# Start addresses of the SBUF tiles in a one-core attention and feed-forward block

## The chip, the cores and the metric

The kernel runs on one core of one Trainium2 chip. The metric is the device time of one execution in microseconds (us), taken as the median of several runs. A profile is one execution, taken by the hardware profiler; its span reaches from the first to the last instruction, and the execution's own time is a little longer than its span.

## The reference

One decoder layer over a sequence of 512 tokens of width 1024, in float32. What is computed, cut to its steps:

```
h    = rms_norm(x)                                   # 512 x 1024
proj = h @ w_in                                      # queries, keys, values and gates of both head groups
A: 4 heads of differential attention: softmax(q1 k1) - lam * softmax(q2 k2), times v, rms_norm
B: 8 heads of sparse attention: compressed blocks + selected blocks + sliding window, mixed by gates
x    = x + rms_norm(concat(A, B) @ w_out)
h    = rms_norm(x)
f    = (silu(h @ w_gate) * (h @ w_up)) @ w_down      # inner width 2816
out  = x + rms_norm(f)
```

With 512 tokens and 8 selectable blocks of which up to 16 are picked, the selected branch and the sliding window both cover the whole causal triangle, so the kernel computes both as plain causal attention.

## The kernel before, in words

Every large product runs on TensorE (PE) in three passes. [...] Weights come from HBM as tiles `wraw` (128x1024, three buffers), ACT makes `whi` (L101, called by `split_w`, L105) and DVE makes `wlo` (L109).

The stages, in order of time:

- Load x, split it into eight `xh` and eight `xl` tiles (L186 to L200).
- Projections: `fm_tile` (L257) holds 24 matmuls of 512 columns into one PSUM bank (L264); `dv_half` and `vg_proj` (L338, L360) have 256 and 280 columns. Rotated queries and keys go to scratch DRAM and come back as `qst` and `kst`.
- Attention heads: scores (L473, L474, with `kst` streamed), softmax on DVE, ACT and POOL, transposes of the probabilities (L489), and the products with the values (L540, L617, L621, with the transposed probabilities `pth`, `ptl`, `pct` streamed).
- Output projection (`mix_part` L664, `mix_final` L676), the residual sum and the second norm, whose transposed result is split into `hth` and `htl` (L807, L808).
- Feed-forward, gate and up (`ff_gate`, L828): for each of 22 blocks of 128 inner columns, 24 matmuls for the gate and 24 for the up half, all in L835.
- Feed-forward, down (`down`, L872): for each of the 22 blocks, 24 matmuls in L874.

[...] In the matmul call the stationary operand comes first and the moving one second:

```
L264  pe.matmul(pt, w[:, k * P:(k + 1) * P], xx[k], ...)                      # moving: xh, xl
L835  pe.matmul(pt, w_col(ww, k), hx[:, k, s0:s1], ...)                       # moving: hth, htl
L874  pe.matmul(acc[i][c], a[f][:, i * P:(i + 1) * P], w[wi][:, c * SEQ:(c + 1) * SEQ], ...)  # moving: whi, wlo
```

For blocks 2 to 21, L835 streams 512 columns at a time (20 x 48 = 960 matmuls); blocks 0 and 1 stream two halves of 256 columns (192 matmuls). The program's order on each engine is set by a scheduler that takes the order of the code, with priorities (`HP`, `HP2`, `HP3`).

SBUF tiles come from pools. A pool takes a stretch of each partition's bytes, and a tile's start follows from what was placed ahead of it, rounded up to 32 bytes. The pools `const`, `weights`, `s` (36 slots of 2048 bytes) and `r` are laid from the low end; `t`, the attention's pool, from the high end; when the attention is done `t` is given back, and `a`, the pool of the feed-forward stage (`hth`, `htl`, the residual `x2`, `silu`, `mixt`), takes its bytes. Small columns (row maxima, row sums, scales, one to 96 floats wide) lie between the wide tiles of `t`.

Of the kernel before, what the change touches and what calls it, by code (L numbers as in the profile page):

```python
# [9 lines left out]
F32 = mybir.dt.float32  # L10
# [7 lines left out]
P = 128  # L18
D_MODEL = 1024
SEQ = 512  # L20
NT = SEQ // P
# [7 lines left out]
NSA_HEADS = 8  # L29
GROUPS = 2  # L30
# [3 lines left out]
NCMP = (SEQ - CMP_BLOCK) // CMP_STRIDE + 1  # L34
NPAD = 32
CMP_HIDDEN = 4 * HEAD_DIM
NLH = CMP_BLOCK // 2
# [40 lines left out]
def hybrid_block_kernel(  # L78
# [8 lines left out]
    def f32(ap):  # L87
        return ap.bitcast(F32)

    cpool = ctx.enter_context(tc.tile_pool(name="const", bufs=1))  # L90
    wpool = ctx.enter_context(tc.tile_pool(name="weights", bufs=3))
    dram = ctx.enter_context(tc.tile_pool(name="scratch", bufs=1, space=bass.MemoryType.DRAM))

    def load_w(src, w=1024):
# [34 lines left out]
    S = ctx.enter_context(tc.tile_pool(name="s", bufs=NS, side="left"))  # L129
    R = ctx.enter_context(tc.tile_pool(name="r", bufs=2, side="left"))  # L130
    tctx = ExitStack()
    T = tctx.enter_context(tc.tile_pool(name="t", bufs=2, side="right"))
    ident = cpool.tile([P, P], F32, name="ident")
    ident_r = T.tile([P, P], F32R, bufs=1, name="ident_r")
    ident_b = T.tile([P, P], BF16, bufs=1, name="ident_b")
    mask_b = T.tile([P, P], BF16, bufs=1, name="mask_b")
    cmask_b = T.tile([P, NT * NPAD], BF16, bufs=1, name="cmask_b")
    sel = T.tile([P, 2 * NCMP], F32, bufs=1, name="sel")
    valid = T.tile([P, 1], F32, bufs=1, name="valid")
    ones = cpool.tile([P, 1], F32, name="ones")  # L140
    gc = cpool.tile([P, NK + 1], F32, name="gc")
    rstd = T.tile([P, NT], F32, bufs=1, name="rstd")
    nrstd = T.tile([P, NT], F32, bufs=1, name="nrstd")
    lam = T.tile([P, 1], F32, bufs=1, name="lam")
    gates = T.tile([P, NT, 3 * NSA_HEADS], F32, bufs=1, name="gates")
    kch = T.tile([P, GROUPS, NPAD], F32R, bufs=1, name="kch")
    kcl = T.tile([P, GROUPS, NPAD], F32R, bufs=1, name="kcl")
    vcs = T.tile([P, GROUPS, HEAD_DIM], F32R, bufs=1, name="vcs")
# [9 lines left out]
    def tslot(name, dt=F32, tag="c"):  # L158
        return T.tile([P, SEQ], dt, tag=tag, name=name, bufs=TAGS[tag])

    def ps(tag, name, dt=F32):
        return PS.tile([P, SEQ], dt, tag=tag, name=name, bufs=PSB[tag])
# [58 lines left out]
    dve.tensor_copy(sel, cst[:, 3 * P:3 * P + 2 * NCMP])  # L221
    dve.tensor_copy(valid, cst[:, 3 * P + 2 * NCMP:3 * P + 2 * NCMP + 1])
    dve.memset(ones, 1.0)
    zero = T.tile([P, GROUPS], F32, bufs=1, name="zero")
    dve.memset(zero, 0.0)
    rp = [sslot(n, F32) for n in ("cos", "sin", "ckv", "skv")]
    cos, sin, ckv, skv = rp
# [16 lines left out]

    lv = sslot("lv", F32)
    nc.sync.dma_start(lv[:, :4 * HEAD_DIM], lamv.partition_broadcast(P))
    l2 = T.tile([P, 2], F32, bufs=1, name="l2")
    for j in range(2):
        dve.tensor_tensor(lv[:, 256 + 64 * j:320 + 64 * j], lv[:, 128 * j:128 * j + 64],
                          lv[:, 128 * j + 64:128 * j + 128], OP.mult)  # L250
# [49 lines left out]
    def load_q(d, m):  # L300
        q = T.tile([P, SEQ], F32R, tag="q", name="qst", bufs=BUFS["q"])
        nc.sync.dma_start(f32(q), d[m].rearrange("d c t -> (d c) t"))
        return q

    def load_k(d, m):
        kk = T.tile([P, 2, SEQ], F32R, tag="k", name="kst", bufs=BUFS["k"])
        src = d[m].rearrange("d (c h) t -> (d c) (h t)", h=2)
        dst = f32(kk).rearrange("(x r) h t -> r x (h t)", r=2)
        for r in range(2):
            nc.sync.dma_start(dst[r], src)  # L310
        return kk
# [63 lines left out]
    def compress(d, v, w1, w2, posd, w2cols):  # L375
        xx = tslot("cx", tag="c")
        nc.sync.dma_start(xx.rearrange("p (g n) -> p g n", g=GROUPS), d[v].rearrange("g d r c n -> (d r c) g n"))
        pos = T.tile([P, NLH], F32, tag="pos", name="pos", bufs=2)
        nc.sync.dma_start(pos, posd.rearrange("(a d) l -> d a l", d=HALF))
        w2t = T.tile([P, 2, w2cols], F32, name=f"w2_{v}", bufs=1)  # L380
        if v:
            nc.sync.dma_start(w2t, w2)
        else:
# [79 lines left out]
    def softmax_map(q, kk, l):  # L463
        ptiles = []
        for grp in ((0, 1), (2,), (3,)):
            st = ps("sc", "sc")
            off = 0
            for i in grp:
                w = (i + 1) * P
                sv = st[:, off:off + w]  # L470
                off += w
                lhs = q[:, i * P:(i + 1) * P]
                pe.matmul(sv, lhs, kk[:, 0, :w], start=True, stop=False)  # L473
                pe.matmul(sv, lhs, kk[:, 1, :w], start=False, stop=False)  # L474
                pe.matmul(sv[:, i * P:], ident_b, mask_b, start=False, stop=True)  # L475
                nm = T.tile([P, 1], F32, tag="nm", name="nm", bufs=8)
                dve.tensor_reduce(nm, sv, AX.X, OP.max, negate=True)  # L477
                pt = T.tile([P, w], F32, tag=f"p{i}", name="p", bufs=PB)
                act.activation(pt, sv, AF.Exp, bias=nm, accum_out=l[:, i:i + 1])  # L479
                ptiles.append(pt)  # L480
        return ptiles
# [14 lines left out]
    def row_mul(eng, p, l):  # L496
        if eng == "p":
            pool.tensor_tensor(p, p, l.to_broadcast(list(p.shape)), OP.mult)  # L498
        elif eng == "a":
            act.activation(p, p, AF.Copy, scale=l)  # L500
        else:
            dve.tensor_scalar(p, p, l, None, OP.mult)

    def new_pt():
        return [T.tile([P, 10, P], F32R, tag="pt" + n, name="pt" + n, bufs=BUFS["pt"]) for n in "hl"]

    def blocks(t, j):
        return t[:, BASE[j]:BASE[j] + NT - j].rearrange("p i q -> p (i q)")
# [9 lines left out]
            nsa_head_(*a)  # L518

    def diff_head_(h, qd, kd, dv):  # L520
        l = T.tile([P, 2, NT], F32, tag="l", name="l", bufs=4)
        pp = []
        for m in range(2):
            mm = 2 * (h % 2) + m
            q, kk = load_q(qd, mm), load_k(kd, mm)
            pp.append(softmax_map(q, kk, l[:, m]))
        dve.reciprocal(l, l)
        dve.tensor_scalar(l[:, 1], l[:, 1], lam, None, OP.mult)  # L528
        pth, ptl = new_pt()
        for i in range(NT):  # L530
            p1, p2 = pp[0][i], pp[1][i]
            row_mul(DSC[i], p2, l[:, 1, i:i + 1])
            dve.scalar_tensor_tensor(p1, p1, l[:, 0, i:i + 1], p2, OP.mult, OP.add)  # L533
        transpose_p(pp[0], pth, ptl)
        av = ps("av", "av")
        n = 0
        for j in range(NT):
            for vi, pt in ((0, pth), (1, pth), (0, ptl)):
                v0 = vi * 256 + (h % 2) * P
                pe.matmul(av[:, j * P:], dv[j][:, v0:v0 + P], blocks(pt, j),  # L540
                          start=(n == 0), stop=(n == 3 * NT - 1))
                n += 1
        o32, sq = tslot("o32", tag="o"), tslot("sq", tag="o")
        act.activation(o32, av, AF.Copy, scale=gc[:, NK:NK + 1])
        act.activation(sq, av, AF.Square)
        ms = ps("tr", "ms")
        for i in range(NT):
            pe.matmul(ms[:, i:i + 1], sq[:, i * P:(i + 1) * P], ones, start=True, stop=True)
        rs = cpool.tile([P, NT], F32, tag="rs", name="rs", bufs=2)
        rsqrt_mean(rs, ms[:, :NT], 1.0 / P)  # L550
        rb = ps(RSB, "rsb")
        for i in range(NT):
            pe.matmul(rb[:, i * P:(i + 1) * P], rs[:, i:i + 1].to_broadcast([P, P]), ident, start=True, stop=True)
        dve.tensor_tensor(sq, o32, rb, OP.mult)
        rs = sq
        oth[h], otl[h] = sslot(f"oh{h}"), sslot(f"ol{h}")
        act.activation(oth[h], rs, AF.Copy, scale=1.0 - LAM_INIT)
        dve.scalar_tensor_tensor(otl[h], rs, 1.0 - LAM_INIT, f32(oth[h]), OP.mult, OP.subtract)

    def cmp_head(h, q, l):  # L560
        g = h // HPG
        st = ps("sc", "scc")
        for i in range(NT):
            o = st[:, i * NPAD:(i + 1) * NPAD]
            pe.matmul(o, q[:, i * P:(i + 1) * P], kch[:, g], start=(i == 0), stop=False)
            pe.matmul(o, q[:, i * P:(i + 1) * P], kcl[:, g], start=False, stop=False)
        pe.matmul(st[:, :P], ident_b, cmask_b, start=False, stop=True)
        sv = st[:, :P].rearrange("p (i n) -> p i n", n=NPAD)
        nm = T.tile([P, NT], F32, tag="nmc", name="nmc", bufs=2)
        bc = [P, NT, NPAD]  # L570
        dve.tensor_reduce(nm, sv, AX.X, OP.max, negate=True)
        c = T.tile([P, P], F32, tag="pc", name="pc", bufs=2)
        cv = c.rearrange("p (i n) -> p i n", n=NPAD)
        dve.tensor_tensor(cv, sv, nm.unsqueeze(2).to_broadcast(bc), OP.add)  # L574
        act.activation(cv, cv, AF.Exp)
        dve.tensor_reduce(l[:, 0], cv[:, :, :NCMP], AX.X, OP.add)
        return c, cv
# [15 lines left out]

    def nsa_head_(h, q, kst, vn, opair):
        g = h // HPG
        l = T.tile([P, 3, NT], F32, tag="l3", name="l3", bufs=4)
        def row_scale(b):
            dve.reciprocal(l[:, b], l[:, b])
            dve.tensor_tensor(l[:, b], l[:, b], gates[:, :, 3 * h + b], OP.mult)
# [284 lines left out]
    for i in range(NT):  # L884
# [3 lines left out]
        u, a, x_ = work("uf"), acc[i], halves(x2[i])  # L888
# [96 lines left out]
```

## Time and profile before

| | |
|---|---|
| median of 3 runs | 717.43 us (714.56 to 718.01) |
| the profiled execution's own time | 715.25 us |
| its span | 713.2 us |
| mean granted TensorE clock | 0.982 |
| PE busy | 683.7 us (96% of the span) |
| DVE busy | 488.3 us (68%) |
| ACT busy | 295.9 us (41%) |
| DMA engines, mean busy share | 35% |

PE is the engine with the highest share, and the share of a whole span is an average over stages. Matmuls overlap one another in the profile (the end of one is modelled, and lies behind the start of the next), so the pace of a stretch of matmuls is read from their starts and their number, not from the duration of one.

### The profile page before, as it was taken

The numbers are of one execution on the slowest core, as the hardware profiler recorded it, in microseconds if no ns is written. First come the engines' busy times: TensorE is split into PE (matmuls) and PEld (weight loads), VectorE is DVE, ScalarE is ACT, GpSimd is POOL, SyncE is SP. The second block draws the span as 40 slices with busy tenths as digits, with TensorE's granted clock in tenths as the row PEclk, the third lists the DMA queues.
The fourth block names the chain that finished last, engine by engine and source line by source line (L and its number), as shares of the span: only waits on it lengthen the run. The fifth ranks groups of instructions, "written<-read, shape, count | busy, mean of one in ns | idle before, by whom it ended". The sixth has DMA issues, their size and how long they took to land.

```text
span 713.2 us, 9399 instructions
## 1 busy us (share of the span) xinstructions
PE 683.7 (96%) x3536; PEld 566.2 (79%) x3536; DVE 488.3 (68%) x803; ACT 295.9 (41%) x612; POOL 63.1 (9%) x74
## 2 busy tenths in 40 slices
PE   7999999999899998987899999999999999999995
PEld 4888878898788877866888888888888888888884
DVE  5777988876999995669586766867667672222227
ACT  7334444466689965435323233232232321121113
POOL 0000000111745434000000000000000000000000
PEclk8999999999999998999999999999999999999999
DMA  8347878551221300470022332223322222322303
GB/s 311 129 133 244 279 238 298 195 191 45 86 78 60 104 16 30 133 251 30 1 90 88 105 102 89 89 88 93 111 92 89 88 91 94 111 89 88 110 8 119
DMA packets 25980, 83.62 MB, mean 117 GB/s; under 512 B 3408, under 2 KB 4304, under 8 KB 25040
## 3 DMA queue, kind: packets, MB, share of 16 engines
q1 hardware_dynamic: 25936, 83.03, 35.0%
q8 instruction: 28, 0.46, 0.3%
q14 instruction: 16, 0.13, 0.1%
HBM read 73.06 MB, written 9.96 MB: 116 GB/s over the span
## 4 chain that ended last, share of the span: by engine, by line
PE 81%; DVE 12%; ACT 4%; issue 2%; DMA 1%; SPq 0%; DVEq 0%; ACTq 0%
PE gu L835 35%; PE acc L874 15%; PE fm L264 11%; PE tr L489 2%; PE mixp L664 2%; DVE nm L477 2%; PE dv L338 2%; PE vg L360 2%; PE avn L617 2%; PE sc L473 2%; PE sc L474 1%; PE mix L676 1%; PE av L540 1%; DVE p L533 1%; DVE ptl L494 1%
## 5 line engine op out<-in xcount | busy, mean ns | idle before, releaser
L109 DVE TENSOR_TENSOR wlo<-wraw,whi 128x1024 fp32r<-128x1024 f32 (+2 forms) x96 | 116.4, 1214 | 144.8 <-ACT whi L101 95.5
L101 ACT ACTIVATE whi<-wraw 128x1024 fp32r<-128x1024 f32 (+2 forms) x96 | 100.8, 1052 | 215.3 <-PE gu L835 92.0
L835 PE MATMUL gu<-hth,whi 128*128 128x512 f32 (+1 forms) x352 | 86.6, 388 | 0.0
L835 PE MATMUL gu<-htl,whi 128*128 128x512 f32 (+1 forms) x352 | 86.2, 385 | 0.0
L835 PE MATMUL gu<-hth,wlo 128*128 128x512 f32 (+1 forms) x352 | 85.6, 385 | 0.0
L835 PEld LDWEIGHTS gu<-hth,whi 128*128 128x128 f32 x352 | 65.0, 192 | 14.8 <-ACT hth L807 0.3
L835 PEld LDWEIGHTS gu<-htl,whi 128*128 128x128 f32 x352 | 64.3, 188 | 14.7
L835 PEld LDWEIGHTS gu<-hth,wlo 128*128 128x128 f32 x352 | 64.1, 188 | 14.7
L841 DVE RECIPROCAL silu<-silu 128x512 f32<-128x512 f32 (+1 forms) x24 | 74.0, 3085 | 0.7
L498 POOL TENSOR_TENSOR p<-p,l 128x384 f32<-128x384 f32 (+3 forms) x60 | 50.1, 862 | 145.0 <-DVE l L528 88.5
L874 PE MATMUL acc<-whi,ffl 128*128 128x512 f32 x144 | 56.0, 389 | 0.0
L874 PE MATMUL acc<-wlo,ffh 128*128 128x512 f32 x144 | 56.0, 389 | 0.0
L874 PE MATMUL acc<-whi,ffh 128*128 128x512 f32 x144 | 55.9, 389 | 0.0
L479 ACT ACTIVATE p<-sc,nm 128x128 f32<-128x128 f32 (+1 forms) x96 | 50.0, 528 | 10.2 <-DVE nm L477 9.8
L477 DVE TENSOR_REDUCE nm<-sc 128x1 f32<-128x128 f32 (+1 forms) x96 | 42.5, 482 | 11.0 <-PE sc L475 7.8
L264 PE MATMUL fm<-xh,whi 128*128 128x512 f32 x128 | 35.9, 419 | 4.8 <-ACT whi L101 2.9
L493 ACT ACTIVATE pth<-tr 128x384 fp32r<-128x384 f32 (+1 forms) x60 | 31.5, 526 | 17.4 <-PE tr L489 17.2
L473 PE MATMUL sc<-kst,qst 128*128 128x128 f32 (+2 forms) x96 | 35.6, 372 | 1.5 <-DVE pc L574 1.2
L494 DVE TENSOR_TENSOR ptl<-tr,pth 128x384 fp32r<-128x384 f32 (+1 forms) x60 | 34.8, 592 | 3.0 <-ACT pth L493 2.7
L489 PE MATMUL tr<-ident,p 128*128 128x128 f32 x200 | 33.6, 280 | 1.3 <-ACT pct L591 0.7
L264 PEld LDWEIGHTS fm<-xh,whi 128*128 128x128 f32 x128 | 24.9, 199 | 12.3 <-ACT whi L101 5.5
L264 PE MATMUL fm<-xl,whi 128*128 128x512 f32 x128 | 32.6, 391 | 0.0
(219 smaller groups left out, 1186.9 us busy)
## 6 DMA issues: line engine op xcount, KB each, us to landing
wraw<-in_wg SPq DMA_DIRECT2D x22, 512.0 KB, 3.3
wraw<-in_wu SPq DMA_DIRECT2D x22, 512.0 KB, 3.3
wraw<-in_wd SPq DMA_DIRECT2D x22, 512.0 KB, 3.3
wraw<-in_wf SPq DMA_DIRECT2D x16, 512.0 KB, 4.9
qk<-rope SPq DMA_DIRECT2D x7, 1024.0 KB, 5.9
kst<-qk SPq DMA_DIRECT2D x24, 256.0 KB, 4.4
qst<-qk SPq DMA_DIRECT2D x16, 256.0 KB, 2.7
wraw<-in_wo SPq DMA_DIRECT2D x8, 512.0 KB, 4.0
```

Source lines behind the costliest of these rows:

```text
L101: act.activation(dst, src, AF.Copy)
L109: (lo_eng or dve).tensor_tensor(lo[:, :w], raw[:, :w], f32(hi[:, :w]), OP.subtract)
L264: pe.matmul(pt, w[:, k * P:(k + 1) * P], xx[k], start=(n == 0), stop=(n == 3 * NK - 1))
L473: pe.matmul(sv, lhs, kk[:, 0, :w], start=True, stop=False)
L477: dve.tensor_reduce(nm, sv, AX.X, OP.max, negate=True)
L479: act.activation(pt, sv, AF.Exp, bias=nm, accum_out=l[:, i:i + 1])
L489: pe.transpose(tr[:, n * P:(n + 1) * P], pts[i][:, j * P:(j + 1) * P], ident)
L494: dve.tensor_tensor(ptl[:, sl], trv, f32(pth[:, sl]), OP.subtract)
L498: pool.tensor_tensor(p, p, l.to_broadcast(list(p.shape)), OP.mult)
L835: pe.matmul(pt, w_col(ww, k), hx[:, k, s0:s1], start=(n == 0), stop=(n == 3 * NK - 1))
L841: dve.reciprocal(sl, sl)
L874: pe.matmul(acc[i][c], a[f][:, i * P:(i + 1) * P], w[wi][:, c * SEQ:(c + 1) * SEQ], start=(first and n == 0), stop=(last and n == 2))
```

## The change

The change moves tiles to other addresses and does nothing else. A pad of 64 bytes (`cpad`) goes into the `const` pool, which moves all tiles of `weights`, `s` and `r`. A pool `edge` with a pad of 224 bytes (`zpad`) is laid at the high end, so that `a` begins lower. A pool `u` takes the small columns out of `t`.

```diff
     cpool = ctx.enter_context(tc.tile_pool(name="const", bufs=1))
+    cpool.tile([P, 16], F32, name="cpad")
     wpool = ctx.enter_context(tc.tile_pool(name="weights", bufs=3))
+    zpool = ctx.enter_context(tc.tile_pool(name="edge", bufs=1, side="right"))
+    zpool.tile([P, 56], F32, name="zpad")
...
     tctx = ExitStack()
+    U = tctx.enter_context(tc.tile_pool(name="u", bufs=1, side="right"))
+    U.tile([P, 32], F32, name="upad")
     T = tctx.enter_context(tc.tile_pool(name="t", bufs=2, side="right"))
...
-    sel = T.tile([P, 2 * NCMP], F32, bufs=1, name="sel")
-    valid = T.tile([P, 1], F32, bufs=1, name="valid")
+    sel = U.tile([P, 2 * NCMP], F32, bufs=1, name="sel")
+    valid = U.tile([P, 1], F32, bufs=1, name="valid")
...
-                nm = T.tile([P, 1], F32, tag="nm", name="nm", bufs=8)
+                nm = U.tile([P, 1], F32, tag="nm", name="nm", bufs=8)
```

In the same way `rstd`, `nrstd`, `lam`, `gates`, `zero`, `l2`, `pos`, `w2_0`, `w2_1`, `l`, `l3` and `nmc` go from `T` to `U`. The starts of the tiles, as the two built programs have them, in bytes above a multiple of 256:

| tiles | pool | before | after |
|---|---|---|---|
| `wraw`, `whi`, `wlo` | weights | 192 | 0 |
| `xh`, `xl`, `dv`, `vn`, `oh`, `ol`, `ws`, `ffh`, `ffl` | s | 192 | 0 |
| `rope` (also the last `ffh`, `ffl`) | r | 192 | 0 |
| `xraw`, `kst`, `pct`, `cst`, `kch`, `vcs` | t | 96 | 0 |
| `qst`, `p`, `pth`, `ptl`, `opair` | t | 160 | 0 |
| `pc` | t | 224 | 0 |
| `hth`, `htl`, `x2`, `gain`, `mixt`, `u`, `silu`, `uf`, `junk` | a | 224 | 0 |
| `ident` (128x128) | const | 160 | 224 |

A slice of such a tile that starts a multiple of 64 columns into it keeps the tile's number, so the moving operands named above start where their tiles start. The lists of instructions of all five engines are the same in both programs, in the same order. What differs is a handful of semaphore waits at the seam between attention and feed-forward, where the pool `a` takes other bytes of `t`: the load of the first gain row waits for a later matmul (the one for which the second gain row, next in SP's queue, waits in both programs), and some waits on loads of `qst` and `kst` stand at other instructions of ACT and DVE.

## Rows read from the trace of the kernel before

**Rows 1.** The page, section 1: busy us, share and count of each engine.

```profile
PE 683.7 (96%) x3536; PEld 566.2 (79%) x3536; DVE 488.3 (68%) x803; ACT 295.9 (41%) x612; POOL 63.1 (9%) x74
```

**Rows 2.** The page, section 4: the chain that ended last, by engine and line.

```profile
PE 81%; DVE 12%; ACT 4%; issue 2%; DMA 1%; SPq 0%; DVEq 0%; ACTq 0%
PE gu L835 35%; PE acc L874 15%; PE fm L264 11%; PE tr L489 2%; PE mixp L664 2%; DVE nm L477 2%; PE dv L338 2%; PE vg L360 2%; PE avn L617 2%; PE sc L473 2%; PE sc L474 1%; PE mix L676 1%; PE av L540 1%; DVE p L533 1%; DVE ptl L494 1%
```

**Rows 3.** The chain in order of time: start us, us, what.

```profile
1.65 4.87 DMA wraw<-in_wf
...
38.63 21.80 PE fm L264 x96
...
348.68 237.28 PE gu L835 x1056
585.96 110.20 PE acc L874 x486
```

**Rows 4.** The timeline of PE, gate and up: start us, us, what.

```profile
425.27 2.03 PE L835 MATMUL gu<-htl,whi 128*128 128x512 f32 x8
427.13 2.03 PE L835 MATMUL gu<-hth,wlo 128*128 128x512 f32 x8
...
432.73 2.03 PE L835 MATMUL gu<-hth,wlo 128*128 128x512 f32 x8
434.60 2.03 PE L835 MATMUL gu<-hth,whi 128*128 128x512 f32 x8
...
438.33 2.03 PE L835 MATMUL gu<-hth,wlo 128*128 128x512 f32 x8
```

**Rows 5.** Groups by line and form, PE: form xcount | busy us, mean ns | idle.

```profile
L835 PE MATMUL gu<-hth,wlo 128*128 128x512 f32 x320 | 81.1, 395 | 0.0
L874 PE MATMUL acc<-whi,ffl 128*128 128x512 f32 x144 | 56.0, 389 | 0.0
```

**Rows 6.** Single lines, PE: count, duration ns min/median/max, first and last start, forms.

```profile
L264 PE MATMUL fm<-xl,whi x128: 389/389/476, 15.8 to 128.3; 128*128 128x512 f32 x128
L621 PE MATMUL avn<-pct,vcs x8: 392/398/405, 188.4 to 298.7; 128*64 128x512 f32 x8
L338 PE MATMUL dv<-whi,xl x64: 279/283/365, 25.6 to 147.8; 128*128 128x256 f32 x64
L835 PE MATMUL gu<-hth,ws x64: 277/283/415, 331.5 to 361.7; 128*128 128x256 f32 x64
```

**Rows 7.** Windows: us; busy PE, PEld, DVE, ACT, POOL; clock; DMA share; GB/s.

```profile
39.00:60.00 21.00, 21.00 (x94) 17.39 (x93) 14.92 (x24) 7.32 (x12) 0.00 (x0) 1.00 0.49 145
400.00:580.00 180.00, 180.00 (x773) 144.57 (x773) 128.74 (x112) 54.07 (x65) 0.00 (x0) 1.00 0.29 94
425.27:427.13 1.86, 1.86 (x9) 1.50 (x8) 1.86 (x1) 0.00 (x0) 0.00 (x0) 1.00 0.66 198
432.60:434.60 2.00, 2.00 (x10) 1.59 (x9) 0.00 (x0) 1.06 (x1) 0.00 (x0) 1.00 0.31 119
```

**Rows 8.** The chain from 125 to 330 us, by line.

```profile
by line: PE tr L489 7.6%; PE mixp L664 7.0%; DVE nm L477 6.7%; PE vg L360 6.3%; PE avn L617 6.2%; PE sc L473 5.1%; PE sc L474 4.2%; PE mix L676 4.0%; PE av L540 3.5%; DVE p L533 3.1%; DVE ptl L494 3.0%; PE dv L338 2.9%; ACT p L479 2.9%; PE 
```

**Rows 9.** Windows as in rows 7: the attention's middle.

```profile
178.00:285.00 107.00, 100.64 (x661) 82.38 (x660) 93.41 (x238) 81.13 (x241) 53.42 (x60) 0.95 0.20 62
```

**Rows 10.** Groups by form, DVE: 1024 elements from tiles of either pool.

```profile
L109 DVE TENSOR_TENSOR wlo<-wraw,whi 128x1024 fp32r<-128x1024 f32 x93 | 113.6, 1223 | 143.9 <-ACT whi L101 94.6 <-PE gu L835 48.3 <-issue 0.6
L793 DVE TENSOR_TENSOR u<-mixt,gain 128x1024 f32<-128x1024 f32 x4 | 4.9, 1222 | 0.0
```

**Rows 11.** DMA issues: line, count, KB each, median us to landing.

```profile
xraw<-in_xT SPq DMA_DIRECT2D x8, 256.0 KB, 5.8
cos<-in_rope SPq DMA_DIRECT2D x1, 256.0 KB, 5.1
```

**Rows 12.** The timeline at the seam: SP's issue of the gain rows, DVE's first use.

```profile
306.51 0.90 SPq L742 DMA_DIRECT2D gain<-in_grow  x2
314.66 1.23 DVE L793 TENSOR_TENSOR u<-mixt,gain 128x1024 f32<-128x1024 f32 x1
```

More of the change, by code (lines that the diff above doesn't have):

```diff
@@ L137, in hybrid_block_kernel @@
     cmask_b = T.tile([P, NT * NPAD], BF16, bufs=1, name="cmask_b")
-    sel = T.tile([P, 2 * NCMP], F32, bufs=1, name="sel")
-    valid = T.tile([P, 1], F32, bufs=1, name="valid")
+    sel = U.tile([P, 2 * NCMP], F32, bufs=1, name="sel")
+    valid = U.tile([P, 1], F32, bufs=1, name="valid")
     ones = cpool.tile([P, 1], F32, name="ones")
     gc = cpool.tile([P, NK + 1], F32, name="gc")
[L142 to L145, printed above, removed]
+    rstd = U.tile([P, NT], F32, bufs=1, name="rstd")
+    nrstd = U.tile([P, NT], F32, bufs=1, name="nrstd")
+    lam = U.tile([P, 1], F32, bufs=1, name="lam")
+    gates = U.tile([P, NT, 3 * NSA_HEADS], F32, bufs=1, name="gates")
     kch = T.tile([P, GROUPS, NPAD], F32R, bufs=1, name="kch")
@@ L223, in hybrid_block_kernel @@
     dve.memset(ones, 1.0)
-    zero = T.tile([P, GROUPS], F32, bufs=1, name="zero")
+    zero = U.tile([P, GROUPS], F32, bufs=1, name="zero")
     dve.memset(zero, 0.0)
@@ L246, in hybrid_block_kernel @@
     nc.sync.dma_start(lv[:, :4 * HEAD_DIM], lamv.partition_broadcast(P))
-    l2 = T.tile([P, 2], F32, bufs=1, name="l2")
+    l2 = U.tile([P, 2], F32, bufs=1, name="l2")
     for j in range(2):
@@ L377, in compress @@
         nc.sync.dma_start(xx.rearrange("p (g n) -> p g n", g=GROUPS), d[v].rearrange("g d r c n -> (d r c) g n"))
-        pos = T.tile([P, NLH], F32, tag="pos", name="pos", bufs=2)
+        pos = U.tile([P, NLH], F32, tag="pos", name="pos", bufs=2)
         nc.sync.dma_start(pos, posd.rearrange("(a d) l -> d a l", d=HALF))
-        w2t = T.tile([P, 2, w2cols], F32, name=f"w2_{v}", bufs=1)
+        w2t = U.tile([P, 2, w2cols], F32, name=f"w2_{v}", bufs=1)
         if v:
@@ L520, in diff_head_ @@
     def diff_head_(h, qd, kd, dv):
-        l = T.tile([P, 2, NT], F32, tag="l", name="l", bufs=4)
+        l = U.tile([P, 2, NT], F32, tag="l", name="l", bufs=4)
         pp = []
@@ L568, in cmp_head @@
         sv = st[:, :P].rearrange("p (i n) -> p i n", n=NPAD)
-        nm = T.tile([P, NT], F32, tag="nmc", name="nmc", bufs=2)
+        nm = U.tile([P, NT], F32, tag="nmc", name="nmc", bufs=2)
         bc = [P, NT, NPAD]
@@ L595, in nsa_head_ @@
         g = h // HPG
-        l = T.tile([P, 3, NT], F32, tag="l3", name="l3", bufs=4)
+        l = U.tile([P, 3, NT], F32, tag="l3", name="l3", bufs=4)
         def row_scale(b):
```

## The prediction

> **What bounds the kernel now.** I read first which engine the end waits for, then the pace of that engine in each stage. PE is busy for 96% of the span [rows 1] and carries 81% of the chain that ended last, DVE 12%, transfers 1% [rows 2]. Three lines hold most of it: L835 (gate and up) 35%, L874 (down) 15%, L264 (projections) 11%. The chain in order of time shows them as unbroken pieces: 21.80 us with 96 matmuls of L264, 237.28 us with 1056 of L835, 110.20 us with 486 of L874 [rows 3]. Inside these pieces PE waits for nobody, so the time of the kernel there is a number of matmuls times the time from one start to the next, which I call the pitch.
>
> The reader is to see that the pitch is not the same in the three lines, though each matmul has 512 moving columns of the same type:
>
> - L264: 21.80 us / 96 = 227.1 ns [rows 3].
> - L874: 110.20 us / 486 = 226.7 ns [rows 3].
> - L835: seven groups of eight start between 425.27 and 438.33 us (the rows in between are of the same kind), so 13.06 us / 56 = 233.2 ns [rows 4].
>
> The durations say the same: 389 ns for L874 [rows 5] and L264 [rows 6], 395 ns for L835 [rows 5]. [...]
>
> Where do 6.3 ns (233.2 less the mean of the other two, 226.9) come from? Not from the other engines. L264 between 39 and 60 us has DVE busy for 14.92 of 21 us (71%), ACT for 35% and DMA for 0.49; L835 between 400 and 580 us has 72%, 30% and 0.29 [rows 7]. Inside L835 the eight matmuls from 425.27 us took 1.86 us with DVE busy throughout, the eight from 432.73 us 1.87 us with DVE idle [rows 4, 7]. Nor from the stationary operand: `whi` and `wlo` serve L264 and L835 alike. What is left in the layout is where the moving operand starts: `xh`, `xl`, `whi` and `wlo` start 192 bytes above a multiple of 256, which is a multiple of 64; `hth` and `htl` start at 224, an odd multiple of 32. A third moving tile, `pct` at 96 (odd again), takes 398 ns at the median, while `xh` and `xl` at 192 take 389 in L264 [rows 6]. So in this trace the clean cases with a start at an odd multiple of 32 cost 6 to 9 ns more per 512 columns. That is a correlation over a handful of tiles. [...]
>
> **The change part by part.** *Feed-forward, gate and up.* `hth` and `htl` go from 224 to 0. If 0 behaves as 192 does, each of the 960 matmuls with 512 columns (three groups like the 320 of [rows 5]) costs 226.9 instead of 233.2 ns: 960 x 6.3 = 6.0 us less. All of it lies on the chain, since the whole stage is one piece [rows 3]. The cover holds: DVE has 128.74 us of work in 180 us [rows 7], and would have it in about 175, 74%. The bounds are 0 (the start has nothing to do with it) and 960 x 9 = 8.6 us (the distance of `pct`); I take 6.0 because both ends of it come from long clean stretches.
>
> *The 192 matmuls with 256 columns in L835*, at the front of the stage: they have a median of 283 ns, and so have the ones of L338, whose moving tiles stand at 192 [rows 6]. With short rows something else sets the pace, and I take 0; the bound above is 192 x 6.3 = 1.2 us.
>
> *Attention.* `kst`, `pth`, `ptl` and `pct` also leave odd multiples of 32. The lines that stream them, L617, L473, L474 and L540, hold 6.2 + 5.1 + 4.2 + 3.5 = 19.0% of the chain between 125 and 330 us [rows 8], so 39 us; 6.3 / 233.2 = 2.7% of that is 1.1 us. In the middle of this stage DVE is busy for 93.41 of 107 us [rows 9] and is what comes late next, and most of these matmuls have fewer than 512 columns. I take half, 0.5 us, and keep 0 and 1.1.
>
> *Projections, output projection, down.* Their moving tiles go from 192 to 0, both multiples of 64: 0. The transposes stream `ident`, which goes from 160 to 224 and stays off: 0. What 0 does that 192 doesn't is shown by no row; the second and third rival are about that.
>
> *DVE, ACT, POOL.* DVE takes 1223 ns for 1024 elements from the tiles at 192 and 1222 ns from those at 224 [rows 10]: 0.
>
> *Transfers.* They are 1% of the chain, the 4.87 us in which the first weights land [rows 3]. The loads of x, into tiles at 96, land after 5.8 us, that of `cos`, into one at 192, after 5.1 [rows 11]; other traffic explains this as well, but as a bound it is 12% of 4.87 us, so 0 to 0.6 us. I take 0, since the two differ in queueing.
>
> [...]
>
> *The waits at the seam.* The first gain row waits for a matmul that its successor in the queue waited for already; the two were issued within 0.90 us at 306.5 us, and DVE first needs one at 314.66 us [rows 12]. The waits that moved on ACT and DVE are for loads of the attention stage, long landed. 0.
>
> **The sum**: 6.0 + 0.5 = 6.5 us. Against the profiled execution that is 713.2 - 6.5 = 706.7 us of span and 715.25 - 6.5 = 708.7 us; this execution lay 2.2 us below the median of the runs, from which the same sum gives 710.9 us. I predict 710.0 us, between the two. For the case's own range I take the upper bounds together, 8.6 + 1.2 + 1.1 + 0.6 = 11.5 us off the profiled execution's 715.25, and for the other end a step a fifth smaller and nothing else, 4.8 us off the median: 704 to 713.
>
> **The rivals.** *Nothing changes* (717.4 us, chance 0.12). The pitch of L835 would then come from something else that only this line has, for instance that its moving tiles are slices of one 16 KB tile. For it speaks that no tile in the trace changes its start while all else stays; against it, that `pct` is slow too and no such slice [rows 6]. [...]
>
> *Slower: one residue for all* (chance 0.06). [...] Priced by the one step the trace shows, the aligned lines would go from 227 to 233 ns: 528 matmuls of L874, 384 of L264 and 192 of L664 and L676, 1104 x 6.3 = 7.0 us, with L835 gaining nothing: 717.4 + 7.0 = 724 us. It decides if L874's pitch rises above 230 ns. Against it: in L264 and L874 all operands stand at 192 already, with DVE 71% busy in the one, and they are the fast lines [rows 3, 7].
>
> *A larger step* (chance 0.08). If 256 (or 128) is a boundary too, all lines gain once more: 528 + 384 + 192 + 960 = 2064 matmuls x 6.3 = 13.0 us on top, 710.9 - 13.0 = 698 us. [...] Against it: nothing in the trace starts at 0 to show it.
>
> That the change misses its aim is no rival here: the built program has the starts that the table gives.
>
> **How the numbers follow.** The forecast has 0.74, nothing 0.12, slower 0.06, the larger step 0.08. A difference of 0.5% (3.6 us) is about what a measurement of this kernel tells from no change. The forecast passes it unless the gain comes out below 3.6 us, for which I leave 0.05 of its 0.74; with 0.08 of the larger step that makes 0.77 for faster, 0.05 + 0.12 = 0.17 for the same, 0.06 for slower. The range 704 to 717 holds the forecast's own and reaches up into the first rival's, whose runs would lie between 714.6 and 718.0 as those of before did; it leaves out the slower case, the larger step and the top of the first rival.
>
> **What would show it.** Right: L835's pitch between 226 and 228 ns and its durations at 389, the chain's long piece of L835 near 231 us instead of 237.28, L874 and L264 unchanged at 227, DVE's forms unchanged. Wrong: L835 still at 233 (the first rival), L874 above 230 (the second), L264 and L874 below 225 (the third), or L835 at 227 with the 6 us given back as new waits of PE in that stage.

## The result and the profile after

| | before | after |
|---|---|---|
| median of the runs timed side by side | 717.12 us (5 runs, 714.56 to 718.01) | 711.54 us (5 runs, 709.9 to 712.37) |
| ratio, 95% interval | | 0.9923 (0.9899 to 0.9946) |
| the profiled execution's own time | 715.25 us | 712.37 us |
| its span | 713.2 us | 710.4 us |
| mean granted TensorE clock | 0.982 | 0.978 |

The kernel became faster by 0.8%, 5.6 us between the medians. The profiled execution of after is the longest of its five, the one of before lies 1.9 us under its median, so the two traces differ by less than the kernels do.

The page of after, section 1 (busy us, share and count of each engine), answers to [rows 1]. PE has 3.6 us less to do; DVE, ACT and POOL are where they were.

```profile
PE 680.1 (96%) x3536; PEld 568.1 (80%) x3536; DVE 488.3 (69%) x803; ACT 296.1 (42%) x612; POOL 62.7 (9%) x74
```

The chain of after in order of time (start us, us, what) answers to [rows 3]:

```profile
39.02 21.80 PE fm L269 x96
...
66.76 7.46 DMA wraw<-in_wf
...
95.86 4.52 PE fm L269 x14
...
353.85 229.41 PE gu L840 x1056
583.26 110.17 PE acc L879 x486
```

L840 is the L835 of before, L879 its L874, L269 its L264. The long piece of gate and up fell from 237.28 to 229.41 us, 7.87 us; down (110.20 to 110.17) and the long piece of the projections (21.80 to 21.80) stayed. But the long piece starts at 353.85 us and not at 348.68: 5.17 us were lost ahead of it, and the span is 2.8 us shorter, not 7.9.

**The gain.** Groups by line and form in after (form xcount | busy us, mean ns | idle), against [rows 5]: gate and up now takes what down takes. A product is summed from `whi` with `xh`, `whi` with `xl` and `wlo` with `xh` (in gate and up `hth` and `htl` in their place), so the line has three groups of 320.

```profile
L840 PE MATMUL gu<-hth,wlo 128*128 128x512 f32 x320 | 79.0, 389 | 0.0
L879 PE MATMUL acc<-whi,ffl 128*128 128x512 f32 x144 | 56.0, 389 | 0.0
```

The timeline of PE in after (start us, us, what), as in [rows 4]:

```profile
425.34 1.98 PE L840 MATMUL gu<-hth,whi 128*128 128x512 f32 x8
...
438.03 1.98 PE L840 MATMUL gu<-htl,whi 128*128 128x512 f32 x8
```

Seven groups of eight lie between these two starts: 12.69 us / 56 = 226.6 ns, where before had 233.2. The window from 400 to 580 us counts the same thing over the whole stage (columns as in [rows 7]): 796 matmuls in 180 us, 773 before. 180 / 796 = 226.1 ns and 180 / 773 = 232.9 ns, at a clock of 1.00 both times.

```profile
400.00:580.00 180.00, 180.00 (x796) 149.05 (x795) 131.60 (x117) 55.96 (x67) 0.00 (x0) 1.00 0.30 97
```

This count is a better measure of the step than the length of the long piece, because the clock at the front of that piece differs between the two executions. Windows from 350 to 355 us, before and then after, have 0.77 and 1.00 (after's long piece begins inside its window):

```profile
350.00:355.00 5.00, 5.00 (x35) 5.00 (x35) 0.61 (x2) 0.21 (x2) 0.00 (x0) 0.77 0.01 3
...
350.00:355.00 5.00, 3.06 (x23) 2.44 (x22) 4.88 (x10) 1.32 (x4) 0.00 (x0) 1.00 0.00 0
```

**The loss ahead of it.** Windows of after (columns as in [rows 7]), in the projections:

```profile
85.00:95.00 10.00, 6.96 (x40) 5.70 (x39) 9.47 (x17) 5.51 (x10) 0.00 (x0) 1.00 0.55 195
95.00:100.00 5.00, 5.00 (x19) 4.12 (x19) 5.00 (x6) 1.84 (x3) 0.00 (x0) 0.66 0.79 233
```

PE was busy for 6.96 of 10 us, and then the granted clock was 0.66 for 5 us; in the window from 95.60 to 98.20 us it was 0.50. The timeline of PE in after shows it in the starts of a row of matmuls: six from 95.66 to 98.22 us, 427 ns each, where the piece of 96 at a clock of 1.00 has 227.1.

```profile
95.66 2.77 PE L269 MATMUL fm<-xh,whi 128*128 128x512 f32 x6
98.22 2.16 PE L269 MATMUL fm<-xl,whi 128*128 128x512 f32 x8
```

In the profile of before the same ten microseconds had PE busy for 8.63 us and the next five a clock of 1.00. The chain tells how much each part cost. The piece of 14 matmuls at 95.86 us in after is this one in before:

```profile
93.06 3.18 PE fm L264 x14
```

So 2.80 of the 5.17 us were lost before this piece (1.67 of them are PE's missing busy time between 85 and 95 us, 8.63 less 6.96), and 1.34 us in it (4.52 against 3.18), at the lower clock. Another 0.9 us came between the first matmuls of gate and up and the long piece, which begins 18.04 us after them in after and 17.14 us in before. Whether the layout has a hand in this is taken up with the runs of the two kernels again.

### The profile page after: what moved, and what is told of

The parts are those of the page before. It is cut to its first block, busy times and chain, and to the rows that moved or that the text cites. A ratio compares the mean times of both kernels' runs of the same rounds, so it can differ in the third digit from the quotient of the medians.

```text
span 710.4 us, 9399 instructions
## 1 busy us (share of the span) xinstructions
PE 680.1 (96%) x3536; PEld 568.1 (80%) x3536; DVE 488.3 (69%) x803; ACT 296.1 (42%) x612; POOL 62.7 (9%) x74
## 4 chain that ended last, share of the span: by engine, by line
PE 79%; DVE 13%; ACT 4%; issue 2%; DMA 2%; DVEq 0%; SPq 0%; ACTq 0%
PE gu L840 34%; PE acc L879 16%; PE fm L269 10%; PE mixp L669 2%; PE tr L494 2%; PE avn L622 2%; PE dv L343 2%; PE vg L365 2%; DMA wraw<-in_wf 2%; PE sc L478 2%; DVE nm L482 2%; PE sc L479 1%; DVE rope L288 1%; PE mix L681 1%; PE av L545 1%
## 5 line engine op out<-in xcount | busy, mean ns | idle before, releaser
L840 PE MATMUL gu<-hth,whi 128*128 128x512 f32 (+1 forms) x352 | 84.3, 382 | 0.0
L840 PE MATMUL gu<-htl,whi 128*128 128x512 f32 (+1 forms) x352 | 84.2, 380 | 0.0
L840 PE MATMUL gu<-hth,wlo 128*128 128x512 f32 (+1 forms) x352 | 83.5, 379 | 0.0
L840 PEld LDWEIGHTS gu<-hth,whi 128*128 128x128 f32 x352 | 64.9, 191 | 12.7 <-ACT hth L812 0.3
L840 PEld LDWEIGHTS gu<-htl,whi 128*128 128x128 f32 x352 | 64.4, 188 | 12.5
L840 PEld LDWEIGHTS gu<-hth,wlo 128*128 128x128 f32 x352 | 64.2, 188 | 12.5
L879 PE MATMUL acc<-whi,ffl 128*128 128x512 f32 x144 | 56.0, 389 | 0.0
L879 PE MATMUL acc<-wlo,ffh 128*128 128x512 f32 x144 | 56.0, 389 | 0.0
L879 PE MATMUL acc<-whi,ffh 128*128 128x512 f32 x144 | 55.9, 389 | 0.0
L269 PE MATMUL fm<-xh,whi 128*128 128x512 f32 x128 | 37.2, 430 | 4.4 <-DVE chl L410 2.1
L269 PEld LDWEIGHTS fm<-xh,whi 128*128 128x128 f32 x128 | 25.7, 206 | 12.3 <-ACT whi L104 5.1
L269 PE MATMUL fm<-xl,whi 128*128 128x512 f32 x128 | 33.2, 396 | 0.0
```

The costliest lines, as they stand in the source:

```text
L269: pe.matmul(pt, w[:, k * P:(k + 1) * P], xx[k], start=(n == 0), stop=(n == 3 * NK - 1))
L840: pe.matmul(pt, w_col(ww, k), hx[:, k, s0:s1], start=(n == 0), stop=(n == 3 * NK - 1))
```

## The experiments

The theory at the start was the prediction's: PE streams a moving operand more slowly when its tile starts at an odd multiple of 32. The first four kernels were timed beside 19 runs of the kernel before (median 716.72 us, 713.82 to 718.35).

**The changed kernel again** (no edit).

> The changed kernel once more, for a second profile. In its first profile the long piece of gate and up is 7.9 us shorter, but the stages ahead of it took 5.2 us more, most of that after a transfer of projection weights that was waited for 7.46 us near 67 us. If that is the scatter of one execution, the start of the long gate-and-up piece comes back towards 349 us here and the time lies at 709 to 712 us. If the new layout slows the transfers of the projection stage, the piece starts at 353 us or later again.

711.15 us (6 runs), ratio 0.9918 (0.9891 to 0.9945): the result holds. The long piece of gate and up took 230.88 us from 353.39 us, which by the words of the expectation speaks for a cost of the new layout; more on that below.

**Only the pool of hth and htl moved.** The kernel before, and 224 bytes laid above `a`; `hth` and `htl` then start at 0 and the weights stay at 192.

```diff
+    Z = ctx.enter_context(tc.tile_pool(name="z", bufs=1, side="right"))
+    Z.tile([P, 56], F32, name="zp")
     A = ...
```

> Only the feed-forward pool is moved (its tiles from 224 to 0 bytes above a multiple of 256); all else is as before. Theory (the start of the moving operand alone): pitch of gate and up 226.7 ns, durations 389 ns, gain 960 x 6.6 = 6.3 us plus what the 256-column matmuls give, so 709 to 711.5 us. Rival (the gain needs moving and stationary operand at the same place above 256): the stationary tiles stay at 192, so the pitch would stay at 233 ns and the time at 717 us.

712.91 us (8 runs), ratio 0.9956 (0.9930 to 0.9982): faster, by something over half of what the whole change gives (two thirds by the medians). The two intervals overlap, so the times alone don't tell the kernels apart. The groups by form do:

```profile
L837 PE MATMUL gu<-hth,whi 128*128 128x512 f32 x320 | 79.9, 392 | 0.0
L837 PE MATMUL gu<-hth,wlo 128*128 128x512 f32 x320 | 79.7, 391 | 0.0
```

391 to 392 ns lie between 395 and 389, and the long piece, 232.84 us, lies between 237.28 and 229.41. A start at 0 alone doesn't bring the full step, which the first theory did not allow for; nor does it stay at 233 ns, as the rival had it.

**Everything else moved, hth and htl left at 224.** The changed kernel, and 32 bytes more above `a`.

```diff
+    Z = ctx.enter_context(tc.tile_pool(name="z", bufs=1, side="right"))
+    Z.tile([P, 8], F32, name="zp")
     A = ...
```

> The change without its feed-forward part: all other tiles at 0, hth and htl back at 224. Theory: pitch of gate and up 233 ns again, time 716 to 718 us, a gain of 0 to 1 us from attention. Rival (the rest of the new layout costs some 2 to 4 us in the projections): 719 to 721 us, and the gate-and-up piece starts at 352 us or later.

716.93 us (12 runs), ratio 1.0001 (0.9987 to 1.0015). `xh`, the weights, `kst`, `qst`, `pth`, `pct`, `ffh` and all loads have their new starts here, and nothing is gained: gate and up is at 396 ns by form, its long piece at 235.62 us.

```profile
L842 PE MATMUL gu<-hth,wlo 128*128 128x512 f32 x320 | 81.1, 396 | 0.0
```

**Everything on the left moved to an odd multiple of 32.** The kernel before with 32 bytes in the `const` pool: the weights and the pools `s` and `r` go from 192 to 224, `hth` and `htl` stay at 224. By the first theory this had to be slower, since down and the projections would now stream from odd starts.

```diff
     cpool = ctx.enter_context(tc.tile_pool(name="const", bufs=1))
+    cpool.tile([P, 8], F32, name="cpad")
```

> The kernel before with 32 bytes of padding in the const pool: weights, activations and split feed-forward tiles go from 192 to 224, an odd multiple of 32, the attention and feed-forward pools stay. Theory: the lines that stream these tiles with 512 columns (down 528, projections 384, output projection 192 matmuls) go from 227 to 233 ns, 1104 x 6.6 = 7.3 us more, 722 to 725 us; gate and up, whose stationary tiles move too, stays at 233. Rival (the stationary start counts as well): gate and up rises above 236 ns, down above 236. Rival (only gate and up's own tiles are special): nothing changes, 717 us.

710.83 us (6 runs), ratio 0.9911 (0.9886 to 0.9936). It is as fast as the changed kernel, with no wide operand of the feed-forward part at a multiple of 64. Single lines of this kernel (duration ns min/median/max):

```profile
L836 PE MATMUL gu<-htl,whi x352: 281/389/389, 335.9 to 577.2; 128*128 128x512 f32 x160, 128*128 128x256 f32 x16
...
L875 PE MATMUL acc<-wlo,ffh x144: 389/389/389, 579.7 to 676.9; 128*128 128x512 f32 x144
```

Here the first theory fell, and no one of the three expectations had a faster kernel. What the five layouts have in common is the distance between the starts of the two operands, the moving one (512 columns here) and the stationary one (the 128x128 part of a tile that an LDWEIGHTS loads): at (192, 192), (0, 0) and (224, 224) a 512-column matmul takes 389 ns; at (0, 192), 64 apart modulo 256, 391 to 392; at (224, 192) and (224, 0), 32 apart, 395 to 396. That is the second theory.

**Other distances.** Three kernels made from the changed one, with `hth` and `htl` cut out of wider tiles so that they start some bytes above the weights' 0; one execution of each. The edit for 64 and 32 bytes (a float has four):

```diff
-    hth = A.tile([P, NK, SEQ], F32R, name="hth")
-    htl = A.tile([P, NK, SEQ], F32R, name="htl")
+    hth = A.tile([P, NK * SEQ + 64], F32R, name="hth")[:, 16:16 + NK * SEQ].rearrange(...)
+    htl = A.tile([P, NK * SEQ + 64], F32R, name="htl")[:, 8:8 + NK * SEQ].rearrange(...)
```

> The changed kernel with hth 64 and htl 32 bytes above a multiple of 256; whi, wlo and all others stay at 0. First theory (only the moving operand's start, boundary at 64): hth 227 ns, htl 233 ns. Second theory (the distance between the moving and the stationary operand's start decides: 0 gives 226.7, 32 gives 233, 64 gives 229): hth 229 ns, htl 233 ns. Durations 392 and 395 ns by the second.

> The changed kernel with hth 16 and htl 4 bytes above a multiple of 256; whi and wlo stay at 0. First theory: both start off a boundary, 233 ns both. Second theory: says only that a distance other than 0 may cost; if distance matters in steps of 32 bytes, both stay at 226.7 ns.

> The changed kernel with hth 128 bytes above a multiple of 256 and htl at 256, which is 0 again; whi and wlo at 0. First theory: both 227 ns. Second theory: htl 226.7 ns; hth between 226.7 (if the pattern repeats every 128 bytes or less) and 230 ns (if it goes on from 64).

The groups by form, `hth` (from `whi`) and `htl` of each. First 64 and 32 bytes (714.91 us):

```profile
L840 PE MATMUL gu<-htl,whi 128*128 128x512 f32 x320 | 81.3, 396 | 0.0
...
L840 PE MATMUL gu<-hth,whi 128*128 128x512 f32 x320 | 79.7, 391 | 0.0
```

16 and 4 bytes (716.14 us):

```profile
L840 PE MATMUL gu<-htl,whi 128*128 128x512 f32 x320 | 82.1, 398 | 0.0
L840 PE MATMUL gu<-hth,whi 128*128 128x512 f32 x320 | 80.6, 394 | 0.0
```

128 and 256 bytes (711.74 us):

```profile
L840 PE MATMUL gu<-hth,whi 128*128 128x512 f32 x320 | 81.2, 395 | 0.0
...
L840 PE MATMUL gu<-htl,whi 128*128 128x512 f32 x320 | 79.6, 391 | 0.0
```

Every distance tried but a multiple of 256 costs something, 4 bytes the most (398), and the cost doesn't fall with the distance: 64 costs less than 128 (391 to 392 against 394 to 395). 32 and 64 give the values that they gave at other places, within one kernel now, as the second theory said. It had left open whether less than 32 bytes counts; it does. Its guess for 128 missed: it allowed up to 230 ns. From 400 to 580 us this kernel has 779 matmuls, 231.1 ns each; two thirds of them are `hth`'s, and with 226 to 228 ns for `htl`'s third the `hth` ones come to some 233 ns, an estimate, as at 32 bytes. At 256 the median is 389 but the mean 391, with single ones up to 398. Each group of eight `htl` matmuls stands between groups at 128; a third of them at 395 and the rest at 389 would make that mean, an estimate again. And in the changed kernel itself `hth` and `whi` start an odd multiple of 256 apart, as the built program has them, and the operands of down an even multiple; both take 389 ns. So 256 is as good as 0. The times are single runs of kernels whose runs spread over 4 us and more, so they decide nothing; the durations do.

**The kernel before again** (no edit).

> The kernel before, for a second profile of its stages. The gate-and-up pitch is 233 ns again. If the first profile was a fast execution ahead of the feed-forward stage, the long gate-and-up piece starts at 350 to 351 us here instead of 348.68; if the changed kernel's layout really costs the projections 4 us, it starts at 348.7 again.

714.18 us, with the long piece of gate and up at 236.64 us from 348.33 us. It was run for the loss ahead of that piece. Windows of this kernel:

```profile
85.00:95.00 10.00, 7.81 (x45) 6.48 (x44) 9.48 (x17) 6.02 (x11) 0.00 (x0) 1.00 0.53 193
95.00:100.00 5.00, 5.00 (x28) 4.25 (x27) 4.22 (x5) 2.24 (x3) 0.00 (x0) 1.00 0.72 218
```

28 matmuls in the five microseconds in which after had 19. By the expectation the start at 348.33 us speaks for a cost of the new layout, and so does the 352.83 us at which the long piece starts with only `hth` and `htl` left at 224; but that kernel's time, 716.93 us against 716.72, shows no such cost. The kernel with 128 and 256 bytes, whose other tiles stand as in the change, has a clock of 1.00 from 70 to 140 us as well:

```profile
70.00:140.00 70.00, 67.88 (x359) 56.56 (x357) 58.40 (x95) 29.68 (x56) 3.52 (x4) 1.00 0.73 256
```

Its long piece starts at 347.90 us. So the layout doesn't force the loss. A late load of weights is not enough for it either. In after that load's piece of the chain ends at 74.22 us (7.46 us from 66.76) and in the kernel before again at 73.39 (6.35 us from 67.04). With everything on the left at 224 it ends at 74.28 us (7.05 us from 67.23), and there the clock stayed at 1.00 from 70 to 140 us. Nor is it always the same loss: the two kernels that follow also start the long piece late, at 352.38 and 353.07 us, with a clock of 1.00 from 70 to 140 us. In their chains a row of eight `rsb` matmuls takes 0.89 us at 164.30 and 165.27 us and 1.72 us at 276.92 and 278.04; in after such a row takes 1.48 us at 278.75, with a clock of 0.83 from 270 to 290 us, and in the kernel before again 0.89 us at 289.25, with a clock of 1.00 from 250 to 300 us. What makes the clock fall in one execution and not in another stays open.

The timed runs span the same clocks, 0.977 to 0.988 for the changed kernel and 0.978 to 0.989 for the one before, and at the upper end the changed one is ahead: 708.13 and 708.44 us at 0.988 against 714.55 and 713.82 at 0.988 and 0.989. Whether the new layout of pool `t` makes such executions more frequent is open. Of the eight profiles taken with it, the two that follow among them, six start the long piece at 352.4 to 353.9 us and two at 347.9 and 350.0; the four taken with the old one start it at 348.3 to 350.3. The times bound it: the kernel with everything on the left at 224 keeps the old `t` and gains 5.9 us (710.83 against 716.72), the changed kernel beside it gains 5.6; and the kernel with only `hth` and `htl` left at 224 has the ratio 1.0001 (0.9987 to 1.0015), so on average the rest of the layout, with what attention may gain by it, costs some 1 us at most.

**The stationary operand moved alone.** Wherever the kernels above moved `hth`, the distance changed with it. Two kernels move the other side. In the first, only the split weights (and the raw tile beside them) go up by 32 bytes: they are the stationary operand of gate and up and of the projections, and the moving one of down.

```diff
+    w0pool = ctx.enter_context(tc.tile_pool(name="w0", bufs=1))
+    w0pool.tile([P, 8], F32, name="w0pad")
     wpool = ctx.enter_context(tc.tile_pool(name="weights", bufs=3))
+    w1pool = ctx.enter_context(tc.tile_pool(name="w1", bufs=1))
+    w1pool.tile([P, 56], F32, name="w1pad")
```

> The changed kernel with only the split weights (whi, wlo, and their raw tile) moved 32 bytes up, by a pad of 32 bytes below their pool and one of 224 above it; hth, xh, ffh and all else stay at multiples of 256. The weights are the stationary operand of gu and fm and the moving one of acc. Theory of the distance between the two operands' starts: all three forms are now 32 bytes apart, so gu goes from 226.7 to about 233.3 ns a matmul although its moving operand has not moved (960 x 6.6 ns = 6.3 us), acc from 226.7 to about 233 (528 x 6.6 ns = 3.5 us) and fm from 227 to about 233 (up to 2.6 us, less where it waits for loads): 721 to 724 us, slower than the kernel before (716.7). Theory of the moving operand's start alone, as in the prediction: gu stays at 226.7, fm at 227, and only acc rises: about 714.7 us.

721.27 us (4 runs), the kernel before 716.46 us (13 runs), ratio 1.0067 (1.0049 to 1.0084): slower than before, as the distance says, and 6.6 us above what the moving start alone allows. Single lines of this kernel:

```profile
L844 PE MATMUL gu<-htl,whi x352: 277/395/396, 339.6 to 585.8; 128*128 128x512 f32 x160, 128*128 128x256 f32 x16
...
L883 PE MATMUL acc<-whi,ffl x144: 391/395/397, 588.1 to 688.2; 128*128 128x512 f32 x144
...
L273 PE MATMUL fm<-xl,whi x128: 392/395/483, 15.7 to 129.7; 128*128 128x512 f32 x128
```

`htl` hasn't moved from 0, and its matmuls went from 389 to 395 ns. In the chain of this kernel the pieces grew to match: 235.68 us for gate and up.

```profile
38.52 22.41 PE fm L273 x96
...
352.38 235.68 PE gu L844 x1056
588.05 113.88 PE acc L883 x488
```

In the second, only pool `s` goes up by 32 bytes, in the same way: `ffh` and `ffl` of 18 blocks, stationary in down. The last four blocks lie in `rope` tiles, which stay at 0, so one line holds both cases. `xh` and `xl` move too.

```diff
+    s0pool = ctx.enter_context(tc.tile_pool(name="s0", bufs=1, side="left"))
+    s0pool.tile([P, 8], F32, name="s0pad")
     S = ctx.enter_context(tc.tile_pool(name="s", bufs=NS, side="left"))
+    s1pool = ctx.enter_context(tc.tile_pool(name="s1", bufs=1, side="left"))
+    s1pool.tile([P, 56], F32, name="s1pad")
```

> The changed kernel with only the pool s moved 32 bytes up, pads as before: ffh and ffl of 18 of the 22 blocks, the stationary operand of 432 of the 528 matmuls of acc; the other four blocks lie in rope tiles, which stay at 0 and are the control within the same line. xh and xl, the moving operand of fm, move too. Theory of the distance: acc from ffh and ffl of pool s goes from 226.7 to about 233 ns although its moving operand has not moved, acc from rope stays at 226.7, gu stays at 226.7, fm goes to about 233: 432 x 6.6 ns = 2.9 us and 1 to 2.6 us for fm, so 715 to 717 us. Theory of the moving operand's start alone: acc stays at 226.7 throughout, fm goes to 233: 712 to 714 us.

714.73 us (10 runs), ratio 0.9981 (0.9965 to 0.9997), 0.3 us under the range of the distance and 0.7 above that of the moving start alone. The time lies between the two, so the durations decide. Single lines of this kernel:

```profile
L883 PE MATMUL acc<-wlo,ffh x144: 395/396/397, 584.2 to 684.3; 128*128 128x512 f32 x144
L883 PE MATMUL acc<-whi,rope x64: 389/389/393, 684.5 to 705.9; 128*128 128x512 f32 x64
L883 PE MATMUL acc<-wlo,rope x32: 388/389/389, 685.0 to 706.1; 128*128 128x512 f32 x32
```

The same line, the same moving tiles at 0: 396 ns while the stationary tile stands at 32, and 389 from the block on at which it stands at 0. The piece of down grew by 2.9 us, as expected to a tenth; the projections' went from 21.80 to 22.41 us, 233.4 ns a matmul; gate and up, with both operands at 0, stayed:

```profile
38.83 22.41 PE fm L273 x96
...
353.07 230.84 PE gu L844 x1056
583.91 113.05 PE acc L883 x486
```

What is shown: at the same granted clock the pace of 512-column matmuls of this type depends on where the moving and the stationary operand start relative to each other, and either can be moved to change it. Why it does, inside PE, no run shows.

## Why the prediction was right, and where it was wrong

The time (710.0 forecast, 711.54 measured, range 704 to 717) and the sign were right, and so was the stage. The reason given for it was wrong, and that the size came out is luck: the change happened to set right what the prediction had left out.

- **What bounds the kernel**: right. The windows of the projections and of gate and up both have a granted clock of 1.00 [rows 7], and the chain's long piece of gate and up is what moved, and by about its pitch times its number.
- **The sentence that failed**: "Nor from the stationary operand: `whi` and `wlo` serve L264 and L835 alike." They do, but at 192 they stand at the same start as `xh` and 32 bytes from `hth`. What the excluded operand brought was the relation to the moving one. The two fast lines of the trace of before had both operands at 192, so "start at a multiple of 64" and "both at the same start" fitted them equally, and I took the one that names a single tile.
- **The witness that misled**: `pct` at 398 ns [rows 6]. It and its stationary `vcs` both stood at 96, so its slowness seemed to speak for the start alone. In after, with both at 0, the median of these eight matmuls is still 396. They are slow for another reason, which no run looked into. A witness of eight instructions in the middle of attention, with 64 stationary columns where the others have 128, should not have outweighed anything.
- **Gate and up, 6.0 us**: right in size by luck, because the change happens to bring both operands of that line to the same start. 960 x (232.9 - 226.1) = 6.5 us by the windows. The long piece is 5.8 to 7.9 us shorter, comparing its two lengths in the profiles of before (236.64 and 237.28) with the two of the changed kernel (229.41 and 230.88); part of that spread is the clock at the front of the piece, as shown above. With the weights left at 192 the same move of `hth` brought less, 391 to 392 ns, so the term held only for the change as a whole.
- **The 256-column matmuls, 0**: right; the ones of `gu<-htl,ws` have a median of 283 ns in after, 282 and 279 in the two profiles of before and 280 with `hth` and `htl` at 224. They show no gain.
- **Attention, 0.5 us**: not seen. With everything but `hth` and `htl` moved, the ratio is 1.0001, and its interval spans 1 us to either side, so neither 0 nor 0.5 is excluded.
- **Projections, down, DVE, transfers, 0**: right, the first two by their chain pieces, but not because 192 and 0 are both multiples of 64: their two operands had equal starts before and after. DVE's product of 1024 elements stays at 1223 ns [rows 10], and the first load's piece of the chain went from 4.87 to 4.35 us in after and stood at 4.85 in the kernel before again and 4.98 in one with all loads' tiles at 0: no step.
- **The rivals.** *Nothing changes* fell: at a distance of 16 bytes a matmul takes 393 to 394 ns, at 32 bytes 395 to 396, at 0 it takes 389. *One residue for all* had the sign the wrong way round: equal starts are the fast case, and the slow kernel came from taking them apart. Its price was 7.0 us on top of the kernel before, 724 us; unequal starts in all three lines (and in 24 matmuls of the output projection) measured 4.8 us on top of it, 721.27 us. *A larger step* fell: down and the projections stand at 389 ns at 0 as they did at 192.
- **Given back**: the prediction had no term for the clock. In after's own profile 5.17 us went ahead of the long piece, in waits of PE and at the lower clock; this is why these two spans differ by 2.8 us although the long piece is 7.87 us shorter.

## What to carry to other kernels

Where long rows of matmuls of this kind (512 columns, a new stationary tile for each) bound a kernel, look up the start addresses of the moving and the stationary operand together, and lay both at the same start modulo 256 (389 ns here, against 391 to 398 at the other distances tried); that both are round numbers is not what counts, 224 and 224 is as good as 0 and 0 (389 ns both). A reason read from a correlation over three tiles wants a kernel in which the other operand moves before it is believed, and the best one is a line in which both cases stand side by side, as in the last experiment.

## What was not expected of the hardware

- A 512-column matmul stream of this type goes at 226 to 227 ns with both operands at the same start and at 233 ns with 32 bytes between them, at the same granted clock of 1.00. By duration: 0 bytes 389 ns, 64 bytes 391 to 392, 16 bytes 393 to 394, 32 and 128 bytes 394 to 396, 4 bytes 398. 256 bytes are as good as 0.
- At 32 bytes it makes no difference which of the two is moved: 395 to 396 ns either way.
- In one execution PE was busy for 6.96 of 10 us, and a granted clock of 0.66 over the next 5 us followed; in another it was busy for 7.81 of 10, and the clock stayed at 1.00. Executions of one kernel differ by 4 to 5 us (713.82 to 718.35 for the one before), nearly as much as the change gives.
